# A hybrid mLSTM and stick-breaking attention layer: an earlier weight split, an accumulation inside SBUF, and eight low parts by DMA

## The chip, the cores and the metric

The kernel runs on one core of one Trainium2 chip. The metric is the device time of one execution in microseconds, lower is better. TensorE (PE) multiplies matrices, VectorE (DVE) does arithmetic between tensors, ScalarE (ACT) copies and activations, GpSimd (POOL) smaller work, and SyncE (SP) issues most DMAs. POOL can issue DMAs too, among them accumulating ones, which add what they read to what stands at their destination. Each engine works through its own instructions in the order in which the program was written; semaphores between them make one wait for another.

## What is computed

One layer for 512 tokens of width 1024: an RMS norm, one projection into the columns of two mixers and of two gates, an mLSTM, a stick-breaking attention, two projections, a gated merge, an output projection and the residual. Cut to what matters here:

```python
h = rmsnorm(x, norm_w)
proj = jnp.einsum('bsd,de->bse', h, w_in) + b_in
(mq, mk, mv, mi, mf, mo, mz, sq, sk, sv, sz, gates) = jnp.split(proj, split_at, axis=-1)
...
hm = mlstm_chunkwise(to_heads(mq_c, M_HEADS), to_heads(mk_c, M_HEADS),
                     to_heads(mv, M_HEADS), log_i, log_f)
...
qs = rmsnorm(to_heads(sq, SB_HEADS), sb_q_norm_w)
ks_ = rmsnorm(to_heads(sk, SB_HEADS), sb_k_norm_w)
os_ = stick_breaking_attention(qs, ks_, to_heads(sv, SB_HEADS))
...
merged = (g_m * jnp.einsum('bse,ed->bsd', y_m, w_proj_m)
          + g_s * jnp.einsum('bse,ed->bsd', y_s, w_proj_s))
x = x + jnp.einsum('bsd,de->bse', merged, w_out)
```

## The kernel before

**Split numbers.** A float32 product is made of three matmuls (`mm3`): both factors are split into a high part, rounded to the type that PE reads fast, and a low part, the rest. The names end in h or l: hh and hl of the normed input, wh and wl of a weight. For weights ACT writes the high part by a copy, and DVE the low part by subtracting the high part from the raw weight (`split`, L98 to L100). There is a second way: ACT writes the high part as before (L126) and minus the raw weight, rounded in the same way, into wl (L127), and POOL issues a DMA that adds the raw weight to it in SBUF (L128). A unit takes it if `by_dma` is set, which the last eight units of w_proj_m do.

**Units.** Weights pass in units of 512 KB. The main loop goes over them by number c. At c the two units behind it have been split (`AHEAD`) and the four behind it have been loaded (`LOADS`). Raw units lie in `stg`, a tile of three buffers, so that unit n+3 can be loaded only when unit n's raw weight is no longer read. All of these loads are on SP's queue, in order, and beside them other DMAs, among them the `az<-ay` pieces of an attention head (L542): sixteen small transfers between two tiles, in two groups of eight. A callback with a due number (`later`, `at_unit`, `Pair.at`) is run at the start of its c, ahead of the splits for that c. Engines hold their instructions in the order in which this loop comes to them.

**Which units.** Units 0 to 3 are the first q group. Units 4 to 17 are the first `Pair`, 18 to 31 the second; 32 to 35 a z group, 36 to 39 q and 40 to 43 k of the second set of attention heads, 44 onward the next groups. In the code E is 32.

**Pairs.** A pair makes two 512-column blocks of the projection in seven products instead of eight (Strassen and Winograd), order p = 1, 2, 6, 5, 7, 3, 4, each in two `Half` units g. It holds raw quarters of the weight: X (B11), Z (B21), Y (B12), V (B22). Sums are made in place: `t3` adds B22 to Y by an accumulating DMA out of DRAM (L999), `t2` adds Y to X on DVE (L1004), `t4` adds X to Z (L1008), `t1` subtracts V from X (L1012). X and Y lie in buffers of tag A, four of them, which the attention heads later use for `ay` and `ty`. `Half.split` (L930) splits its quarter, and for p = 1 of the first pair, units 4 and 5, it takes the way by DMA (L936 to L938). Results leave PSUM through ACT (`u`, L1024), DVE (`dst`, L1033) and an accumulating DMA on POOL's queue (`dst<-u`, L1036).

**At the start** ACT also makes copies h of the transposed normed input (L337), sixteen of 128 by 128 for token blocks 2 and 3, from which the forms of the pair are made (L905). Later, in a set of heads, `qraw` and `kraw` are evicted from PSUM by DVE (L387), squared by ACT (`sqj`, L404), and transposed by DVE into `ty` (L431), which takes a buffer of tag A.

Of the kernel before, what the change touches and what calls it, by code (L numbers as in the profile page):

```python
# [12 lines left out]
OP = mybir.AluOpType  # L13
# [14 lines left out]
E = 4 + 14 * PAIRS  # L28
# [9 lines left out]
def tile_hybrid_layer(  # L38
# [16 lines left out]
    nc = tc.nc  # L55
# [21 lines left out]
    def blk(tag, dt=F32, shape=(512,), name=None, p=128):  # L77

        where = mp if tag in MISC else sp
        return where.tile([p] + list(shape), dt, name=name or tag, tag=tag, bufs=BUFS[tag])  # L80
# [17 lines left out]
    def split(src, hi, lo):  # L98
        nc.scalar.activation(hi, src, AF.Copy)  # L99
        nc.vector.tensor_tensor(lo, src, hi.bitcast(F32), op=OP.subtract)  # L100


    class Unit:


        def __init__(self, src, c0, rows=None):
            if rows is None:
                self.ap = src[:, c0:c0 + 128].rearrange("(k p) c -> p k c", p=128)
                self.shape = [KT, 128]
            else:  # L110
                self.ap = src[rows:rows + 256, c0:c0 + 512].rearrange("(k p) c -> p k c", p=128)
                self.shape = [2, 512]
            self.slow = None
            self.heavy = False
            self.by_dma = False
# [5 lines left out]
        def split(self):  # L121
            self.wh = blk("wh", FR, self.shape)
            self.wl = blk("wl", FR, self.shape)
            if self.by_dma:

                nc.scalar.activation(self.wh, self.st, AF.Copy)  # L126
                nc.scalar.activation(self.wl, self.st, AF.Copy, scale=-1.0)  # L127
                nc.gpsimd.dma_start(out=self.wl, in_=self.st, accum_op=OP.add)  # L128
            else:
                split(self.st, self.wh, self.wl)  # L130

    units = []
# [225 lines left out]
    class SbSet:  # L358
# [105 lines left out]
        def head(self, h):  # L464
            hs = slice(h * 128, (h + 1) * 128)
            tr = []
            for name in ("q", "k"):
                th, tl = own = two("qk", FR, name=name + "tt")
                if (name, self.s, h // 2) in TURNED:
                    tp = self.tz[name, h // 2][:, h % 2].rearrange("p a (i j) -> p i a j", j=32)  # L470
                    th, tl = [x.rearrange("p (i a j) -> p i a j", a=4, j=32) for x in own]
                else:
                    tp = att_ps()
                    for tb in range(TB):
                        nc.tensor.transpose(tp[:, tb * 128:(tb + 1) * 128], self.raw[name][tb][:, hs], ident)
                if name == "q" and not (name, self.s, h // 2) in TURNED:
                    nc.scalar.activation(th, tp, AF.Copy, scale=qkw)
                    nc.vector.scalar_tensor_tensor(tl, tp, qkw, th.bitcast(F32), op0=OP.mult, op1=OP.subtract)
                else:
                    split(tp, th, tl)  # L480
                tr.append(own)
# [69 lines left out]
            def turn(js):  # L551
                n0, n1 = slot[js[0], js[0]], slot[TB - 1, js[-1]] + 1
                at = (n1 - n0) * 128
                ah, al = blk("y", FR, name="ath"), blk("y", FR, name="atl")
                split(az[:, :, n0:n1, :].rearrange("p b i j -> p i b j"),
                      *[x[:, 0:at].rearrange("p (i b j) -> p i b j", b=4, j=32) for x in (ah, al)])
                for j in js:
                    o, n = (slot[j, j] - n0) * 128, T - j * 128
                    a_parts[j] = ah[:, o:o + n], al[:, o:o + n]
# [348 lines left out]
    def h_form(row, col):  # L908
        def sta(k, tb):
            c = slice(256 * row + 128 * tb, 256 * row + 128 * tb + 128)  # L910
            return hh[:, 4 * col + k, c], hl[:, 4 * col + k, c]
        return sta

    def s_form(f):
        def sta(k, tb):
            c = slice(128 * tb, 128 * tb + 128)
            return form[f][0][k // 2][:, k % 2, c], form[f][1][k // 2][:, k % 2, c]
        return sta

    class Half:  # L920
# [7 lines left out]
            pass  # L928

        def split(self):  # L930
            self.wh = blk("wh", FR, (2, 512))
            self.wl = blk("wl", FR, (2, 512))
            name = {1: "X", 2: "Z", 6: "X", 5: "X", 7: "Y", 3: "V", 4: "Z"}[self.p]
            x = self.pair.raw[name, self.g]
            if self.pair.base == 4 and self.p == 1:
                nc.scalar.activation(self.wh, x, AF.Copy)  # L936
                nc.scalar.activation(self.wl, x, AF.Copy, scale=-1.0)
                nc.gpsimd.dma_start(out=self.wl, in_=x, accum_op=OP.add)  # L938
            else:
                split(x, self.wh, self.wl)  # L940
# [19 lines left out]
    class Pair:  # L960

        def __init__(self, c1, c2, got1, got2):
            self.c = {1: c1, 2: c2}
            self.got = {1: got1, 2: got2}
            self.raw, self.bank, self.dst = {}, {}, {}
            self.sta = {1: h_form(0, 0), 2: h_form(0, 1), 6: s_form(6), 5: s_form(5),
                        7: s_form(7), 3: s_form(3), 4: h_form(1, 1)}
            b = self.base = len(units)
            for p in (1, 2, 6, 5, 7, 3, 4):
                for g in range(2):  # L970
                    units.append(Half(self, p, g))
            first = b == 4
            for g in range(2):
                if first:
                    plan = {"X": g, "Z": g, "V": 2 + g, "Y": 1}
                else:
                    plan = {"X": b - 8 + g, "Z": b - 8 + 6 * g, "V": b - 4 + g, "Y": b - 6 + g}
                for name, c in plan.items():
                    self.at(c, self.load, name, g)
                self.at(b + g - 1 if first else b + g - 3, self.t3, g)  # L980
                self.at(b + 1 + g, self.t2, g)
                self.at(b + 3 + g, self.t4, g)
                self.at(b + 4 + g, self.t1, g)
            self.at(b + 1, self.rows)
# [10 lines left out]
            nc.sync.dma_start(t, w_in[r:r + 256, c:c + 512].rearrange("(k p) c -> p k c", p=128))  # L995

        def t3(self, g):
            r, c = 512 + 256 * g, self.c[2]
            nc.gpsimd.dma_start(out=self.raw["Y", g], accum_op=OP.add,  # L999
                                in_=w_in[r:r + 256, c:c + 512].rearrange("(k p) c -> p k c", p=128))  # L1000

        def t2(self, g):
            x, y = self.raw["X", g], self.raw["Y", g]
# [60 lines left out]
    def at_unit(c, fn, *a):  # L1064
        later.setdefault(c, []).append(lambda: fn(*a))

    for f in (5, 7, 6):
        for i in range(2):
            at_unit(2, form_sum, f, i)
# [124 lines left out]

    chan_group(w_proj_m, 0, D, lambda k: ymp[k], pm_evac)
    n_proj = len(units)
    for un in units[n_proj - 8:]:
        un.by_dma = True


# [170 lines left out]
    for g in range(2):  # L1371
        at(-15 + 2 * g, w_load, "B22", g, "P5")
        at(-14 + 2 * g, w_load, "B12", g, "A")
        at(-11 + 2 * g, w_load, "B11", g, "A")
        at(-11 + 2 * g, t3, g)
        at(-7 + 2 * g, t2, g)
        at(-6 + 2 * g, t1, g)
        at(1 + g, t4, g)
# [115 lines left out]
    for c in range(N):  # L1494
# [34 lines left out]
        for e in list(pend):  # L1529
            if c >= e[0] and e[2]():  # L1530
                pend.remove(e)
                g = e[3]()
# [36 lines left out]
```

## Time and profile before

| | |
|---|---|
| median of 3 runs | 705.02 us (703.99 to 705.18) |
| the profiled execution | 705.31 us, its span 703.6 us |
| mean granted clock of PE | 0.988 of full speed |
| HBM read, written | 71.46 MB, 5.30 MB |
| 76 low parts on DVE (wl<-stg) | 93.0 us busy, 1224 ns each |
| 8 low parts by DMA (wl<-stg) | 5.9 us from issue to landing, median |

In a list of waits a row has the engine, what waited and its line, an arrow to what ended the wait, and then the total in us, how often, and the longest. In a timeline a row begins with the start and the length in us, and a bracket at its end says how long the engine had been idle and what ended that. A window has the busy time of PE, the granted clock (PEclk), the DMA share, and GB/s; the share is packet time over the time of sixteen engines, and goes past 1 where packets overlap.

### The profile page before, as it was taken

Reading aid. Unit: us, or ns where it says so; the run is one execution under the profiler, and the core shown is the slowest. Engines: PE = TensorE matmul, PEld = TensorE weight load, DVE = VectorE, ACT = ScalarE, POOL = GpSimd, SP = SyncE. Lnnn points to the kernel's source line nnn. Section 1 sums busy time; section 2 is a strip of 40 time slices with the busy share of each in tenths; the row PEclk is TensorE's granted clock in tenths of the full one; section 3 lists DMA queues with packets and bytes.
Section 4 is the critical chain, followed back from the end, with each engine's and each line's share of the span. In section 5 each row is a group of like instructions: output and inputs, shape, how many; then the busy total and the mean of one; then the engine's idle time right before and its main releaser. Section 6 shows DMA issues by size and latency. Waiting matters only on the chain.

```text
span 703.6 us, 9522 instructions
## 1 busy us (share of the span) xinstructions
PE 681.4 (97%) x3114; PEld 563.8 (80%) x3114; DVE 499.0 (71%) x857; ACT 367.7 (52%) x697; POOL 147.5 (21%) x308
## 2 busy tenths in 40 slices
PE   8988989999979999999999999999999999999997
PEld 5866867888768888888887888888888888888876
DVE  6858678787686876698998446599734365545896
ACT  7656436654736554564445664444647452444461
POOL 4023416542545421130001031100001200111020
PEclk9989999999998999999999999999999999999999
DMA  6775965735343456525455424334432335989433
GB/s 245 262 143 152 247 169 116 186 87 173 81 125 97 115 177 178 155 61 150 92 101 143 134 61 120 82 101 133 109 101 69 92 118 148 301 182 220 129 79 102
DMA packets 127666, 97.33 MB, mean 138 GB/s; under 512 B 19658, under 2 KB 105060, under 8 KB 127616
## 3 DMA queue, kind: packets, MB, share of 16 engines
q1 hardware_dynamic: 121104, 83.48, 41.7%
q0 software_dynamic: 6368, 13.11, 10.0%
q8 instruction: 24, 0.39, 0.2%
q14 instruction: 26, 0.21, 0.1%
q10 hardware_dynamic: 144, 0.13, 0.1%
HBM read 71.46 MB, written 5.30 MB: 109 GB/s over the span
## 4 chain that ended last, share of the span: by engine, by line
PE 64%; DVE 9%; issue 5%; DMA 4%; ACT 3%; SPq 2%; POOL 1%; DVEq 0%; POOLq 0%; ACTq 0%
PE dps L94 17%; PE dps L96 17%; PE dps L95 17%; PE aps L95 2%; PE aps L96 2%; PE aps L94 2%; DVE acc L724 2%; SPq L542 2%; DMA Y<-in_w_in_dram 2%; PE dps L953 2%; DVE wl L100 1%; DMA stg<-in_w_in_dram 1%; PE aps L953 1%; ACT sqj L404 1%; DVE tmp L730 1%
## 5 line engine op out<-in xcount | busy, mean ns | idle before, releaser
L94 PE MATMUL dps<-hh,wh 128*128 128x512 f32 x448 | 176.6, 394 | 5.1 <-DVE kraw L387 4.5
L96 PE MATMUL dps<-hh,wl 128*128 128x512 f32 x448 | 175.5, 392 | 0.6 <-DVE wl L100 0.6
L95 PE MATMUL dps<-hl,wh 128*128 128x512 f32 x448 | 175.3, 391 | 0.0
L100 DVE TENSOR_TENSOR wl<-stg,wh 128x1024 fp32r<-128x1024 f32 x76 | 93.0, 1224 | 65.3 <-ACT wh L99 64.8
L94 PEld LDWEIGHTS dps<-hh,wh 128*128 128x128 f32 x448 | 84.7, 189 | 22.4 <-issue 4.9
L96 PEld LDWEIGHTS dps<-hh,wl 128*128 128x128 f32 x448 | 84.6, 189 | 19.4 <-DVE wl L100 1.4
L99 ACT ACTIVATE wh<-stg 128x1024 fp32r<-128x1024 f32 x76 | 80.0, 1052 | 37.9 <-PE dps L95 11.2
L95 PEld LDWEIGHTS dps<-hl,wh 128*128 128x128 f32 x448 | 84.8, 189 | 16.8
L94 PE MATMUL dps<-wh,hh 128*128 128x512 f32 x96 | 37.6, 392 | 1.3 <-DVE qraw L387 1.3
L727 ACT ACTIVATE tmp<-acc 128x512 f32<-128x512 f32 x16 | 10.1, 633 | 52.3 <-DVE acc L724 52.3
L96 PE MATMUL dps<-wh,hl 128*128 128x512 f32 x96 | 37.4, 390 | 0.0
L95 PE MATMUL dps<-wl,hh 128*128 128x512 f32 x96 | 37.4, 390 | 0.0
L724 DVE SCALAR_TENSOR_TENSOR acc<-tmp,vec,acc 128x511 f32<-128x511 f32 (+2 forms) x48 | 36.0, 750 | 1.7
L500 POOL TENSOR_SCALAR_AFFINE_SELECT om<-om 128x128 f32<-128x128 f32 x32 | 14.1, 439 | 83.6 <-ACT om L498 83.6
L786 POOL TENSOR_SCALAR_AFFINE_SELECT w_all<-om 128x128 f32<-128x128 f32 x16 | 7.4, 492 | 109.2 <-DMA om<-rb_d 109.1
L506 DVE TENSOR_TENSOR_SCAN om<-om 128x512 f32<-128x512 f32 (+3 forms) x32 | 26.6, 831 | 4.4 <-POOL om L500 4.4
L441 POOL DMA_DIRECT2D tz<-ty x48 | 25.9, 549 | 9.2 <-PE aps L953 5.0
L96 PE MATMUL dps<-yh,wl 128*128 128x512 f32 x64 | 25.0, 390 | 0.0
L95 PE MATMUL dps<-yl,wh 128*128 128x512 f32 x64 | 24.9, 389 | 0.0
L94 PE MATMUL dps<-yh,wh 128*128 128x512 f32 x64 | 24.9, 389 | 0.0
L498 ACT ACTIVATE om<-aps,rq 128x512 f32<-128x512 f32 (+3 forms) x32 | 16.9, 527 | 13.3 <-PE aps L96 12.2
L843 ACT ACTIVATE hns<-aps,hst 128x256 f32<-128x256 f32 x16 | 7.6, 475 | 29.8 <-DVE hst L842 22.6
(303 smaller groups left out, 1553.1 us busy)
## 6 DMA issues: line engine op xcount, KB each, us to landing
stg<-in_w_in_dram SPq DMA_DIRECT2D x71, 512.0 KB
az<-ay SPq DMA_DIRECT2D x128, 40.0 KB
stg<-in_w_proj_s_dram SPq DMA_DIRECT2D x8, 512.0 KB
B<-in_w_out_dram SPq DMA_DIRECT2D x8, 512.0 KB
stg<-in_w_proj_m_dram SPq DMA_DIRECT2D x8, 512.0 KB
wl<-stg POOLq DMA_DIRECT2D x8, 512.0 KB, 5.9
dst<-u POOLq DMA_DIRECT2D x12, 256.0 KB, 5.7
X<-in_w_in_dram SPq DMA_DIRECT2D x4, 512.0 KB
```

The costliest lines, as they stand in the source:

```text
L94: nc.tensor.matmul(ps, ah, bh, start=first, stop=False)
L95: nc.tensor.matmul(ps, ah, bl, start=False, stop=False)
L96: nc.tensor.matmul(ps, al, bh, start=False, stop=last)
L99: nc.scalar.activation(hi, src, AF.Copy)
L100: nc.vector.tensor_tensor(lo, src, hi.bitcast(F32), op=OP.subtract)
L441: q.dma_start(tz[32 * b:32 * b + 32, :, a, :], src[32 * a:32 * a + 32, b])
L498: nc.scalar.activation(om[:, 0:n], zp, AF.Sigmoid, scale=rn[:, h:h + 1])
L500: nc.gpsimd.affine_select(out=om[:, ts], in_=om[:, ts], compare_op=OP.is_gt, fill=1.0, base=0, channel_multiplier=1, pattern=[[-1, 128]])
L506: nc.vector.tensor_tensor_scan(back, back, back, 1.0, op0=OP.mult, op1=OP.bypass)
L542: nc.sync.dma_start(az[32 * a:32 * a + 32, b, :, :], ay[32 * b:32 * b + 32, a, :, :])
L724: nc.vector.scalar_tensor_tensor(acc[:, j:], t[:, 0:T - j], cw(3 - j, ch), acc[:, j:], op0=OP.mult, op1=OP.add)
L953: nc.tensor.matmul(pr.bank[key, tb], a, w[:, i, :], start=begin and n == 0, stop=end and n == 2, skip_group_check=again)
```

## The change

It has three parts.

1. `Half.split` does nothing if it has been done. The splits of units 4 and 5 are asked for by callbacks at c = 1 and c = 2.
2. `t3` adds V to Y inside SBUF in place of B22 out of DRAM. For this the first pair loads V at c = g, with X and Z, and not at c = 2 + g; and `t3` is due at b + g - 2 in both pairs: units 2 and 3 in the first (before 3 and 4), units 16 and 17 in the second (before 15 and 16).
3. Units E+4 to E+11, that is 36 to 43, take the way by DMA for their low parts.

```diff
         def split(self):
+            if hasattr(self, "wh"):
+                return
             self.wh = blk("wh", FR, (2, 512))
...
-                    plan = {"X": g, "Z": g, "V": 2 + g, "Y": 1}
+                    plan = {"X": g, "Z": g, "V": g, "Y": 1}
...
-                self.at(b + g - 1 if first else b + g - 3, self.t3, g)
+                self.at(b + g - 2, self.t3, g)
...
         def t3(self, g):
-            r, c = 512 + 256 * g, self.c[2]
-            nc.gpsimd.dma_start(out=self.raw["Y", g], accum_op=OP.add,
-                                in_=w_in[r:r + 256, c:c + 512].rearrange("(k p) c -> p k c", p=128))
+            nc.gpsimd.dma_start(out=self.raw["Y", g], in_=self.raw["V", g], accum_op=OP.add)
...
+    for g in range(2):
+        at_unit(1 + g, units[4 + g].split)
...
-    for un in units[n_proj - 8:]:
+    for un in units[n_proj - 8:] + units[E + 4:E + 12]:
         un.by_dma = True
```

Where it moves instructions is seen in the engines' own order. First ACT near the start, before the change; L337 are the h copies (the last eight rows of two are those of token blocks 2 and 3), L936 and L937 the split of a unit of the first pair:

```order
L337 ACTIVATE h_356<-aps,nw_t 128x128 x2
L337 ACTIVATE h_359<-aps,nw_t 128x128 x2
L936 ACTIVATE wh<-X 128x1024
L937 ACTIVATE wl<-X 128x1024
L936 ACTIVATE wh<-X 128x1024
L937 ACTIVATE wl<-X 128x1024
```

and ACT in the same place of the changed kernel, where these lines are L938 and L939:

```order
L337 ACTIVATE h_286<-aps,nw_t 128x128 x2
L337 ACTIVATE h_289<-aps,nw_t 128x128 x2
L938 ACTIVATE wh<-X 128x1024
L939 ACTIVATE wl<-X 128x1024
L337 ACTIVATE h_349<-aps,nw_t 128x128 x2
L337 ACTIVATE h_352<-aps,nw_t 128x128 x2
...
L337 ACTIVATE h_365<-aps,nw_t 128x128 x2
L337 ACTIVATE h_368<-aps,nw_t 128x128 x2
L938 ACTIVATE wh<-X 128x1024
L939 ACTIVATE wl<-X 128x1024
```

Unit 4's two copies now stand ahead of the sixteen h copies of token blocks 2 and 3; unit 5's stand behind them, where unit 4's stood.

POOL from the first pair to the second, as a difference (rows of the norms between them left out); `wl<-X` are the low parts of units 4 and 5, `Y<-` the accumulations of `t3`, `dst<-u` those of the pairs' results:

```order
-L938 DMA wl<-X 128x1024 x2
-L999 DMA Y<-in_w_in_dram 128x2x512 x2
...
-L1036 DMA dst<-u 128x512 x2
-L999 DMA Y<-in_w_in_dram 128x2x512
-L1036 DMA dst<-u 128x512 x2
-L999 DMA Y<-in_w_in_dram 128x2x512
...
+L940 DMA wl<-X 128x1024
+L1000 DMA Y<-V 128x1024
+L940 DMA wl<-X 128x1024
+L1000 DMA Y<-V 128x1024
...
+L1036 DMA dst<-u 128x512 x4
+L1000 DMA Y<-V 128x1024 x2
```

In the first pair one `Y<-V` now stands ahead of unit 5's low part; in the second pair both stand behind four `dst<-u`, where each stood behind two.

The third place is DVE at units 42 and 43 (k of the second set), before the change; `wl` is a unit's low part, `ay`, `om` and `a_all` belong to an attention head:

```order
L387 TENSOR_TENSOR qraw<-dps,brow 128x512 x4
L100 TENSOR_TENSOR wl<-stg,wh 128x1024
L100 TENSOR_TENSOR qtt<-tz,qtt 128x512
L100 TENSOR_TENSOR ktt<-tz,ktt 128x512
L100 TENSOR_TENSOR wl<-stg,wh 128x1024
L524 STREAM_TRANSPOSE ay<-a_all 128x4x32 x5
```

and POOL at the same place of the changed kernel, where the two low parts are now issued; L282 to L411 are the norms of q:

```order
L411 TENSOR_SCALAR rq<-rq 128x4
L128 DMA wl<-stg 128x1024
L282 TENSOR_SCALAR rq<-ssq 128x4
L283 TENSOR_TENSOR rq<-rq,mhalf 128x4
L411 TENSOR_SCALAR rq<-rq 128x4
...
L128 DMA wl<-stg 128x1024
L499 MEMSET om 128x1
```

Both `wl` rows are gone from DVE. SP's order around units 42 and 43 is the same before and after: a load, eight `az<-ay`, a bias row, a load, eight `az<-ay`; what frees the `stg` buffer of each load is now the end of a low part's DMA instead of a DVE instruction.

## The prediction

> **What bounds the kernel now.** I read the page's head first, then the list of what TensorE (PE) waited for, then the timelines of the engines around each wait.
>
> ```profile
> span 703.6 us, 9522 instructions
> PE 681.4 (97%) x3114; PEld 563.8 (80%) x3114; DVE 499.0 (71%) x857; ACT 367.7 (52%) x697; POOL 147.5 (21%) x308
> PE dps L94 <- DVE kraw L387: 4.5, 1, 4.5
> PE aps L953 <- DVE wl L100: 3.7, 3, 2.4
> PE dps L953 <- DMA wl<-X: 2.9, 1, 2.9
> PE dps L953 <- DVE wl L100: 1.0, 2, 0.8
> ```
>
> PE is busy for 97% of the span, and the change takes no matmul away. So the time can move only at PE's few holes: what each lasts, and what it does to the clock afterwards. The rows (total, times, longest) say what ended the largest: one wait of 4.5 us for VectorE (DVE) evicting kraw, three of 3.7 us together for low parts made on DVE, one of 2.9 us for a low part made by DMA, and two of 1.0 us together for DVE again. I call the places gap 1 (the DMA, at 36 us), gap 2 (58 us, DVE low parts), gap 3 (97 to 108 us, several short ones, second pair) and gap 4 (kraw, 206 us). All sums are against the profiled execution, 705.31 us (span 703.6 and 1.7 around it); it lies 0.3 above the median of 705.02. 0.2% of it, 1.4 us, is about what a measurement of this kernel can tell from no change.
>
> **Gap 1: unit 4's low part (edit 1).** Rows of ACT, of POOL, of PE, and PE's windows (busy, granted clock, DMA share, GB/s):
>
> ```profile
> 24.51 1.14 ACT L337 ACTIVATE h<-aps,nw_t 128x128 f32<-128x128 f32 x4 [3.60 <-DVE hl L325]
> 29.79 1.15 ACT L337 ACTIVATE h<-aps,nw_t 128x128 f32<-128x128 f32 x4 [0.61 <-DVE hl L325]
> 30.80 1.08 ACT L936 ACTIVATE wh<-X 128x1024 fp32r<-128x1024 f32 x1
> 31.75 1.07 ACT L937 ACTIVATE wl<-X 128x1024 fp32r<-128x1024 f32 x1
> 33.15 1.04 POOL L938 DMA_DIRECT2D wl<-X  x1 [16.18 <-ACT wl L937]
> 35.23 0.39 PE L1448 MATMUL dps<-fl,hh 128*128 128x512 f32 x1
> 35.46 0.39 PE L953 MATMUL dps<-wh,hh 128*128 128x512 f32 x1
> 38.77 0.80 PE L953 MATMUL dps<-wl,hh 128*128 128x512 f32 x1 [2.93 <-DMA wl<-X]
> 37.00:38.00 1.00, 0.00 (x0) 0.96 0.93 172
> 38.00:39.00 1.00, 0.23 (x1) 0.50 1.10 197
> 44.00:45.00 1.00, 1.00 (x4) 0.63 1.05 236
> ```
>
> Unit 4's split (L936, L937) stands behind sixteen h copies, so its DMA leaves at 33.15 and lands at about 38.7. Matmuls follow each other by 0.23 us: PE could have gone on at 35.46 + 0.23 = 35.69 and went on at 38.77, 3.1 us later. The clock fell just before 38.0 and was still 0.63 on average in the last window shown: full speed from 44.74. The 6.0 us from 38.77 to 44.74 ran at half speed, another 3.0 lost. **Gap 1 costs about 6.0 us.**
>
> The move puts unit 4's two copies into ACT's idle 3.60 us before 24.51. X of half 0 must be in by then:
>
> ```profile
> DMA packets 1521, 2.94 MB, mean 294 GB/s; under 512 B 98, under 2 KB 98, under 8 KB 1519
> GB/s 410 467 410 377 369 385 385 385 410 410 401 418 426 401 385 393 393 385 410 401 434 418 393 393 418 401 393 254 197 172 98 49 25 33 25 16 0 0 0 0
> ```
>
> This is 24 to 34 us in forty slices: the pair's eight loads of 0.52 MB run at about 400 GB/s, 1.3 us each, until 31. Of their 4.2 MB some 1.3 had moved before 24, so X0, first in the queue, is there by about 24. The copies then end by 26, and the h copies, which before waited 0.6 us between groups for DVE, absorb the rest. The DMA leaves at about 26 and takes, amid loads, 5.6 us as before or somewhat more: 32 to 34.5, ahead of 35.69. That hole closes.
>
> What is late next is unit 5. Its split now stands directly behind the h copies, where unit 4's stood: copies 30.8 to 32.8, DMA at 33.15. Unit 5 starts on PE at 35.46 + 12 x 0.227 = 38.2 and needs its low part one matmul later, at 38.4. With the 5.6 us of gap 1's DMA it lands at 38.75; it now has Y<-V of half 0 ahead of it on POOL's queue, and the second one behind it, so I let it land between 38.7 and 40.2, and take a wait of 1.0. No hole of PE of 1.5 us or less in this trace is followed by half clock. **Gain 5.0 us**, between 3.5 (wait of 2.5, clock still full) and 6.0 (no wait).
>
> The Trainium skill, "TensorE: Matmul & The Clock Gate", section "What's actually happening", has the clock fall after at least one idle window, about 3.4 us. By that rule gap 1, idle for 2.9, would never have lost its clock, would cost 3.1 alone, and the sum below would come out 2.9 us higher. The trace disagrees: 0.50 stands in the window from 38.00 after 2.3 us of idleness, so I go by the rows.
>
> **Gap 2 (nothing).** This chain is DVE's own:
>
> ```profile
> 50.82 1.23 DVE L100 TENSOR_TENSOR wl<-X,wh 128x1024 fp32r<-128x1024 f32 x1 [0.26 <-ACT wh L99]
> 60.11 1.22 DVE L100 TENSOR_TENSOR wl<-X,wh 128x1024 fp32r<-128x1024 f32 x1
> ```
>
> Between the two DVE has no idle time; the work is timed by unit 6's start, not by Y's arrival. It moves as a block with PE: 0, apart from 1.5 either way for where half clock falls. V0 and V1 loaded earlier delay X1 by one load, 1.3 us, to about 29, still ahead of its split at 30.8. The removed DRAM read of Y's addend is 2 MB less traffic over both pairs and no time by itself.
>
> **Gap 3 (edit 2 in the second pair).** The chain of waits and the rows around it:
>
> ```profile
> 81.59 13.13 DMA Y<-in_w_in_dram
> 94.82 1.23 DVE L1004 TENSOR_TENSOR X<-X,Y 128x1024 f32<-128x1024 f32 x1 [4.38 <-DMA Y<-in_w_in_dram]
> 76.57 1.89 POOL L999 DMA_DIRECT2D Y<-in_w_in_dram  x1
> 80.45 1.78 POOL L1036 DMA_DIRECT2D dst<-u  x2 [2.00 <-DVE dst L1033]
> 89.00:91.00 2.00, 2.00 (x10) 1.00 1.15 220
> ```
>
> The second accumulation takes 13.1 us and holds DVE for 4.4, which costs PE at least 2.3 us in short holes (the 3.7 of the list without gap 2's 2.4, and the 1.0). Reading from SBUF spares the DRAM side, and the packets are larger. But both accumulations now stand behind all four dst<-u, so the first leaves at about 81.6, not 76.57, and both then share a DMA system that is full (share 1.15). The second lands between 92.8 and 96 against 94.73. I take 0.3 gained; bounds: 2.3 gained (all that PE pays for), 1 lost (landing at 96).
>
> **Gap 4: eight low parts by DMA (edit 3).** Rows of DVE, SP, PE and ACT, then how the late stage, which already does this, fares:
>
> ```profile
> 186.02 1.22 DVE L100 TENSOR_TENSOR wl<-stg,wh 128x1024 fp32r<-128x1024 f32 x1 [2.59 <-ACT wh L99]
> 187.27 0.37 SPq L119 DMA_DIRECT2D stg<-in_w_in_dram  x1
> 187.75 4.97 SPq L542 DMA_DIRECT2D az<-ay  x8
> 193.44 0.39 SPq L119 DMA_DIRECT2D stg<-in_w_in_dram  x1
> 193.88 5.28 SPq L542 DMA_DIRECT2D az<-ay  x8
> 200.55 1.42 DVE L431 STREAM_TRANSPOSE ty<-qraw 128x256 f32<-128x256 f32 x4 [1.48 <-DMA az<-ay]
> 209.95 2.48 DVE L387 TENSOR_TENSOR kraw<-dps,brow 128x512 f32<-128x512 f32 x4
> 210.78 0.76 PE L94 MATMUL dps<-hh,wh 128*128 128x512 f32 x1 [4.50 <-DVE kraw L387]
> 184.94 1.04 ACT L99 ACTIVATE wh<-stg 128x1024 fp32r<-128x1024 f32 x1
> L127 ACT ACTIVATE wl<-stg x8: 1041/1041/1047, 607.6 to 645.7; 128x1024 fp32r<-128x1024 f32 x8
> DMA to landing us min/median/max: 4.8/5.9/8.9
> SPq L119 <- DMA wl<-stg: 29.2, 5, 6.9
> ```
>
> Eight DVE subtractions of 1.22 go, 9.8 us, but PE waits for none of them; eight ACT copies of 1.04 and eight DMAs come. What matters is the stg slot: the load three units on takes it when the low part is done, now when the DMA **lands**. On SP's queue that load stands ahead of the az pieces, and DVE's ty reuses the buffer that those pieces read; DVE waited 1.48 us for them and then ran without a break to kraw, for which PE waited 4.5. The chain SP, az, ty, kraw, PE has no slack left.
>
> Step by step: unit 42's high part ends at 185.98, its negative copy about 1.0 later, its DMA leaves at 187.35 and lands 4.8 to 5.9 later, at 192.1 to 193.2. The load that stood at 187.27 slips by 4.9 to 5.9. The eight az issues follow (5.0), brow (0.6), and the second load, which then finds unit 43's DMA (copies end at 193.1, landing at 198.3 to 199.4) just done. The whole row slips by 5 to 6 us, ty with it, and PE restarts at about 216.4 instead of 210.78: **5.6 lost**, bounds 5.0 and 6.5. The eight DMAs themselves come in time: unit 42 is needed at 194.1, unit 43 at 200. In the late stage SP lost 29.2 us in five such waits, up to 6.9 each, so the wait is real. The longer hole also leaves the clock down: on average 0.2 more.
>
> ACT takes the eight copies between 150 and 193, where it is idle for whole waits; were that cover gone, unit 42's DMA would leave a copy, 1 us, later, and the slip would be 6.6.
>
> **Sum:** 705.3 - 5.0 (gap 1) + 0 (gap 2) - 0.3 (gap 3) + 5.6 + 0.2 (gap 4) = 705.8 in a profiled execution, 705.5 beside the median.
>
> **The rivals.**
> - *Forecast, 0.45:* gap 1's gain is eaten by gap 4. Its own range is 703.0 to 708.5: faster 0.07, same 0.22, slower 0.16.
> - *Early and light transfers win, 0.27:* unit 5's DMA, at the shortest landing, misses nothing (6.0 gained instead of 5.0), and SBUF accumulation empties the queue, so gap 3 goes too (2.3 instead of 0.3). 705.5 - 1.0 - 2.0 = 702.5, down to 701 if the az pieces slip only by 4. For it: a 512 KB low part took 4.8 us where traffic was light. Against it: DMA share above 1 where both sit. All faster.
> - *Unit 5 breaks the clock again, 0.20:* its DMA shares POOL's queue with Y<-V and the remaining loads. If it lands later than about 40.5, PE idles for over 2 us as before and half clock follows; gap 1 returns 1 to 2 us in place of 5.0, and the time is 709 to 710. For it: Y<-in took 9.6 to 13.1 us in that queue. All slower. The Trainium skill, "DMA: Bandwidth & Descriptors", section "Queues, rings and completion order", says that an engine takes turns between queue rows by packet, so the loads would not merely go first; no row here shows the turns.
> - *Edit 2 doesn't do what it says, 0.08:* the second accumulation lands after 96, since it now shares the queue with the first from its start; gap 3 grows by 1 to 2, 707 to 708. Slower 0.06, same 0.02.
>
> For that 13.1 and the 9.6:
>
> ```profile
> DMA to landing us min/median/max: 9.6/11.3/13.1
> ```
>
> Chances: faster 0.07 + 0.27 = 0.34, same 0.22 + 0.02 = 0.24, slower 0.16 + 0.20 + 0.06 = 0.42. The range runs from 700.0 to 710.5: it leaves out the corners, unit 42 at the 8.9 us landing (PE itself would wait and the row slip by 9) and at the lower end it goes a little past the faster rival's 701.
>
> **What would show it.** Right: no half clock between 38 and 45 us, and a wait of about 1 us or less at unit 5's first low matmul; DVE's first X<-X,Y of the second pair later than 87.6 relative to unit 18; SP waiting at L119 for a wl<-stg landing near 188 (all 5 us earlier by the clock), az and ty 5 to 6 us later against PE's unit 42, and a kraw wait near 10 us. Wrong: PE's kraw wait stays near 4.5, or the clock falls in the first pair, or gap 3's holes are gone.

## The result and the profile after

| | before | after |
|---|---|---|
| median, runs on the same chips | 704.50 us (703.75 to 705.38, n = 6) | 708.33 us (707.26 to 709.90, n = 6) |
| profiled execution, its span | 705.31 us, 703.6 us | 707.75 us, 706.0 us |
| ratio after / before | | 1.0056 (95%: 1.004 to 1.0072) |

The change makes the kernel slower by 0.56%, 0.40 to 0.72%; the forecast was 705.5 us with a range of 700.0 to 710.5. Ratios here are estimated from all timed executions and can differ a little from the quotient of the medians; one execution of e4 below, at 1130.1 us, is left out of its ratio. The list of PE's waits in the changed kernel (total, times, longest), to be held against the one of before:

```profile
PE dps L94 <- DVE kraw L387: 10.4, 1, 10.4
PE aps L955 <- DVE wl L100: 3.8, 3, 2.4
PE dps L955 <- DMA wl<-X: 2.2, 1, 2.2
```

Gap 4 grew from 4.5 to 10.4 us. The wait for a low part by DMA in the first pair is still there, 2.2 instead of 2.9 us, but it is now unit 5's. The two waits of 1.0 us on L953's DVE low parts are gone from the list, and gap 2's row is nearly as it was (before 3.7 us in three waits, now 3.8).

Gap 1 in the changed kernel, POOL's and PE's timelines and one of PE's windows (busy, granted clock, DMA share, GB/s):

```profile
25.45 1.06 POOL L940 DMA_DIRECT2D wl<-X  x1 [8.84 <-ACT wl L939]
28.27 0.87 POOL L1000 DMA_DIRECT2D Y<-V  x1 [1.75 <-DMA Y<-in_w_in_dram]
33.07 0.85 POOL L940 DMA_DIRECT2D wl<-X  x1 [3.93 <-ACT wl L939]
35.45 0.39 PE L955 MATMUL dps<-wl,hh 128*128 128x512 f32 x1
40.53 0.50 PE L955 MATMUL dps<-wl,hh 128*128 128x512 f32 x1 [2.20 <-DMA wl<-X]
41.00:42.00 1.00, 1.00 (x6) 1.00 0.93 190
```

Unit 4's low part is in time: its first low matmul runs at 35.45 without a wait. Unit 5's DMA leaves at 33.07 as forecast, but is in only at about 40.5, 7.4 us later. The clock stays at 1.00 behind that wait in this execution.

Gap 4, SP's, DVE's and PE's timelines and SP's list of waits:

```profile
188.76 5.91 SPq L542 DMA_DIRECT2D az<-ay  x8
195.40 0.37 SPq L119 DMA_DIRECT2D stg<-in_w_in_dram  x1
195.82 5.40 SPq L542 DMA_DIRECT2D az<-ay  x8
202.62 1.42 DVE L431 STREAM_TRANSPOSE ty<-qraw 128x256 f32<-128x256 f32 x4 [5.59 <-DMA az<-ay]
212.84 0.76 PE L94 MATMUL dps<-hh,wh 128*128 128x512 f32 x1 [10.37 <-DVE kraw L387]
SPq L119 <- DMA wl<-stg: 51.9, 10, 9.2
```

PE runs 3.8 us earlier than before when it reaches this stage, and yet the first az group leaves 1.0 us later (188.76 against 187.75) and the second 1.9 later. DVE's ty waits 5.59 us for them, before 1.48. SP's waits for a low part's landing have grown from 5 to 10 and from 29.2 to 51.9 us.

Gap 3, DVE's timeline:

```profile
87.40 1.23 DVE L1004 TENSOR_TENSOR X<-X,Y 128x1024 f32<-128x1024 f32 x1 [2.86 <-DMA Y<-V]
91.00 1.23 DVE L1004 TENSOR_TENSOR X<-X,Y 128x1024 f32<-128x1024 f32 x1 [1.24 <-DMA Y<-V]
```

The first X<-X,Y now waits as well (2.86 us), the second less (1.24, before 4.38). PE's lead over the kernel of before grows from 3.0 to 3.8 us over gap 3.

Matmul by matmul the starts in the two profiled executions differ by: -5.7 us after gap 1's place, -3.5 after unit 5's wait, -3.0 after gap 2, -3.8 after gap 3, +2.1 after gap 4, and +2.4 at the last one.

### The profile page after: what moved, and what is told of

Read it like the earlier page. It is cut to its first block, busy times and chain, and to the rows that moved or that the text cites. A ratio compares the mean times of both kernels' runs of the same rounds, so it can differ in the third digit from the quotient of the medians.

```text
span 706.0 us, 9541 instructions
## 1 busy us (share of the span) xinstructions
PE 678.5 (96%) x3114; PEld 562.3 (80%) x3114; DVE 490.1 (69%) x849; ACT 375.6 (53%) x705; POOL 151.8 (21%) x316
## 3 DMA queue, kind: packets, MB, share of 16 engines
q1 hardware_dynamic: 121104, 83.48, 40.5%
## 4 chain that ended last, share of the span: by engine, by line
PE 62%; DVE 9%; DMA 7%; issue 5%; ACT 4%; SPq 2%; POOL 0%; DVEq 0%; ACTq 0%; POOLq 0%
PE dps L96 17%; PE dps L94 17%; PE dps L95 17%; PE aps L95 2%; PE aps L96 2%; PE aps L94 2%; DMA wl<-stg 2%; DVE acc L724 2%; DMA stg<-in_w_in_dram 2%; DMA Y<-V 2%; SPq L542 2%; PE dps L955 2%; DVE wl L100 1%; PE aps L955 1%; DMA az<-ay 1%
## 5 line engine op out<-in xcount | busy, mean ns | idle before, releaser
L94 PE MATMUL dps<-hh,wh 128*128 128x512 f32 x448 | 176.5, 394 | 10.9 <-DVE kraw L387 10.4
L100 DVE TENSOR_TENSOR wl<-stg,wh 128x1024 fp32r<-128x1024 f32 x68 | 83.4, 1226 | 56.1 <-ACT wh L99 55.7
L99 ACT ACTIVATE wh<-stg 128x1024 fp32r<-128x1024 f32 x68 | 71.6, 1052 | 29.4 <-PE dps L95 10.9
L94 PE MATMUL dps<-wh,hh 128*128 128x512 f32 x96 | 37.6, 392 | 1.3 <-DVE qraw L387 1.3
L128 POOL DMA_DIRECT2D wl<-stg x16 | 14.3, 892 | 94.5 <-DVE yml L100 40.0
L126 ACT ACTIVATE wh<-stg 128x1024 fp32r<-128x1024 f32 x16 | 16.9, 1058 | 28.4 <-PE dps L95 16.9
L500 POOL TENSOR_SCALAR_AFFINE_SELECT om<-om 128x128 f32<-128x128 f32 x32 | 16.0, 506 | 58.3 <-ACT om L498 58.1
```

Of the source, the lines that this page charges most:

```text
L94: nc.tensor.matmul(ps, ah, bh, start=first, stop=False)
L500: nc.gpsimd.affine_select(out=om[:, ts], in_=om[:, ts], compare_op=OP.is_gt, fill=1.0, base=0, channel_multiplier=1, pattern=[[-1, 128]])
```

## The experiments

Nine kernels, each against the kernel of before on the same chip. The medians of before beside them were 703.2 to 703.9 us, so ratios are compared, not microseconds from one comparison to another. Column "unit 5" is PE's wait for unit 5's low part (in the kernels without edit 1, unit 4's), "kraw" the wait at gap 4, both in the profiled execution.

| kernel | ratio to before (95%) | unit 5 | kraw |
|---|---|---|---|
| changed kernel | 1.0056 (1.004 to 1.0072) | 2.2 | 10.4 |
| e1: edits 1 and 2 | 0.9974 (0.9959 to 0.9989) | 2.3 | 4.8 |
| e2: edit 3 alone | 1.0099 (1.008 to 1.0117) | 2.1 | 10.4 |
| e3: edit 1 alone | 0.9959 (0.9945 to 0.9973) | none | 4.4 |
| e4: all, six units by DMA | 0.9979 (0.9966 to 0.9991) | 2.0 | 5.0 |
| e5: e1, Y<-V behind both low parts | 0.9948 (0.9935 to 0.9960) | none | 4.6 |
| e6: all, unit 42 only | one execution, 707.29 us | 2.2 | 9.7 |
| e7: all, unit 43 only | one execution, 709.10 us | 1.8 | 9.9 |
| e8: all, az pieces first | 0.9998 (0.9984 to 1.0012) | 2.2 | 5.7 |
| e9: e5, az pieces first | 0.9915 (0.9899 to 0.9932) | none | 3.1 |

**e1, the first two edits.** Against the changed kernel:

```diff
-    for un in units[n_proj - 8:] + units[E + 4:E + 12]:
+    for un in units[n_proj - 8:]:
```

> Edits 1 and 2 without edit 3 (units 36 to 43 keep their low parts on DVE). Theory S (edit 3 costs through SP's queue: the load three units on waits for the landing, the az pieces stand behind it): the kraw wait returns from 10.4 to about 4.5 us and the time is 3.5 to 4.5 us under before, 0.994 to 0.995. Rival D (the lengthened kraw wait comes from the earlier edits, since everything ahead of it runs 3.8 us earlier and DVE or the transfers do not follow): the kraw wait stays at 8 us or more and the time is within 0.2% of before.

The kraw wait is 4.8 us, so its growth comes from edit 3 and not from what runs ahead of it; D falls. The profiled span is 700.4, 3.2 under the profiled one of before, but by the ratio the gain is only 0.26%, 1.8 us, about half of what was expected. Its twelve executions spread from 699.3 to 704.3; e4 and e5 below bear on that.

**e2, edit 3 alone** (the same line the other way, on the kernel of before).

> Edit 3 alone on the kernel of before. Theory S: the kraw wait is 10 to 10.5 us, the gaps of the pairs are as before, and the time is 5.5 to 6.5 us over before, 1.008 to 1.009. Rival D: the kraw wait is below 6 us and the time within 0.3% of before.

10.4 us and 1.0099: S, by the ratio a little above the 1.009 that it expected, by the medians (6.05 us over before) inside. Edit 3 alone loses more than the whole change does. This run also shows how much gap 1 varies: its first pair is that of the kernel of before, and yet PE waited 2.08 us there and not 2.93, and half clock lasted 3.4 us and not 6.8 (37.6 to 41.0, against 37.9 to 44.7). Reckoned as in the prediction, gap 1 cost some 4 us in this execution and not 6.0.

**e3, edit 1 alone.** The guard in `Half.split` and the two `at_unit` calls on the kernel of before, with both accumulations behind both low parts on POOL's queue.

> Edit 1 alone: the early split of unit 4, the accumulations still out of DRAM and, on POOL's queue, behind both low parts. Theory Q (unit 5's 2.2 us wait in the changed kernel comes from the Y<-V that shares the queue ahead of its low part): unit 5's low part lands at 38.7 to 39.5, PE waits 0.3 to 1.0 us there, and the time is 5 to 6 us under before, 0.992 to 0.993. Rival L (the loads still in flight delay it): the wait stays near 2 us and the time is about 3.5 us under before, 0.995.

Unit 5's wait is gone: the low part was issued at 32.79 and landed 5.7 us later (the shortest in the view of tile X), in time. So the wait follows Q. The gain is 0.41%, less than the 0.7 to 0.8% expected, and the traces show two things that took from it. A hole opens 10 us on: unit 8's low part on DVE comes 1.02 us late, behind an X<-X,Y before which DVE had stood idle (the profile names no releaser there; its Y, summed out of DRAM, is the likely one):

```profile
48.49 0.50 PE L955 MATMUL dps<-wl,form 128*128 128x512 f32 x1 [1.02 <-DVE wl L100]
```

And the 5 to 6 us were taken from one profiled execution of before, of 705.3 us, in which gap 1 cost 6.0; the median of before beside e3 is 703.2, and e2's execution shows gap 1 at some 4. e3's five times, 699.4 to 700.5, lie close together.

**e4, six units by DMA.** Against the changed kernel:

```diff
-    for un in units[n_proj - 8:] + units[E + 4:E + 12]:
+    for un in units[n_proj - 8:] + units[E + 4:E + 10]:
```

> The changed kernel with six units by DMA, 36 to 41, and units 42 and 43 on DVE again. Theory S (only the two loads that stand ahead of the az pieces matter, those that wait for units 42 and 43): the kraw wait is 4 to 5 us, and the time is that of edits 1 and 2 alone within 0.2%. Rival G (each of the eight DMAs costs its share, by ACT's copies or by the DMA engines): three quarters of the loss stays, some 4 us over edits 1 and 2 alone.

The kraw wait is 5.0, the ratio that of e1 within 0.05%. Units 36 to 41 by DMA cost nothing and bring nothing that these runs can tell; G falls as a share of each unit. This kernel's profiled execution also shows what the 2 us hole at unit 5 can do. PE's timeline, and PE's windows:

```profile
40.32 0.50 PE L955 MATMUL dps<-wl,hh 128*128 128x512 f32 x1 [1.98 <-DMA wl<-X]
41.00:42.00 1.00, 1.00 (x4) 0.50 1.11 223
```

Here 1.98 us of idleness was followed by half clock, in the changed kernel 2.20 us was not. The kernels with this hole spread (e1 5.0 us over twelve executions, e8 4.3 over twelve), those without it less (e3 1.1 over five, e5 1.7 over six, e9 2.3 over five). Fewer executions spread less in any case, so this is a hint and no proof.

**e5, the order on POOL.** Against e1:

```diff
-                self.at(b + g - 2, self.t3, g)
+                self.at(b + g - 1 if first else b + g - 2, self.t3, g)
```

> Edits 1 and 2 without edit 3, the first pair's Y<-V put behind both low parts on POOL's queue (due one unit later). Theory Q (the Y<-V ahead of it delays unit 5's low part): the 2 us wait at unit 5 is gone, the low part lands within 6.5 us of its issue, and the time is that of edit 1 alone or up to 1.5 us under it (699 to 700.5; its later hole near 48 us closes where Y<-V lands earlier than the DRAM form). Rival L (loads still in flight): the wait stays 1.5 us or more and the time is that of edits 1 and 2.

POOL's timeline (the low part of unit 5, then the first Y<-V) and PE's next wait:

```profile
33.09 0.85 POOL L940 DMA_DIRECT2D wl<-X  x1 [6.26 <-ACT wl L939]
33.64 1.18 POOL L1000 DMA_DIRECT2D Y<-V  x1
47.76 0.50 PE L955 MATMUL dps<-wl,form 128*128 128x512 f32 x1 [0.62 <-DVE wl L100]
```

The low part left at 33.09, as in the changed kernel (33.07), and was in after 5.3 us instead of 7.4. The loads were still in flight here too: their queue moved 0.46 MB from 32 to 36 us, in the changed kernel 0.26. So the Y<-V issued at 28.27 ahead of it, not the loads, made it late in the changed kernel. The median, 699.46, is 0.5% under before, in the band that Q named; the later hole shrank from 1.02 to 0.62 us.

**e6 and e7, one unit by DMA.** `units[E + 10:E + 11]` and `units[E + 11:E + 12]` in the changed kernel's line.

> The changed kernel with the DMA way for unit 42 alone of the eight. Theory S: the load that waits for unit 42 slips about 5 us and everything behind it on SP with it, so the kraw wait is 9 to 10.5 us, nearly all of the loss from one unit. Rival H (the two waits add up, each half): 7 to 8 us. Rival G (ACT's copies): below 5.5.

> The changed kernel with the DMA way for unit 43 alone of the eight. Theory S: the second load, between the two groups of az pieces, waits for unit 43's landing, 4.5 to 5 us after the time at which it stood, and the second group with it: kraw wait 8.5 to 10 us, by itself nearly the whole loss again. Rival H: 7 to 8 us. Rival G: below 5.5.

Rows of the lists of PE's waits, e6 and then e7:

```profile
PE dps L94 <- DVE kraw L387: 9.7, 1, 9.7
PE dps L94 <- DVE kraw L387: 9.9, 1, 9.9
```

Either unit alone makes nearly all of the loss, and both together hardly more: the costs are not a sum. (That is read from the waits; each kernel has one timed execution.) SP's timeline of e7 shows how:

```profile
190.79 0.58 SPq L350 DMA_DIRECT2D brow<-in_b_in_dram  x1
197.02 0.37 SPq L119 DMA_DIRECT2D stg<-in_w_in_dram  x1
197.44 5.02 SPq L542 DMA_DIRECT2D az<-ay  x8
```

With unit 42 on DVE the first group leaves early, SP is through at 191.4, and then stands until 197.0 for unit 43's landing. With unit 42 by DMA it is the first load that stands, and when SP comes to the second, unit 43 is nearly done.

**e8, the az pieces first.** The two loads that wait for units 42 and 43 are issued after the head's generators of their c. Against the changed kernel:

```diff
-        fetch(c + LOADS + 1)
+        if c not in LATE:
+            fetch(c + LOADS + 1)
+
+    LATE = (E + 9, E + 10)
...
+        if c in LATE:
+            fetch(c + LOADS + 1)
         units[c].mm(1)
```

> The changed kernel, all eight by DMA, with the two loads that wait for units 42 and 43 issued behind the az pieces that stood behind them. Theory S: ty no longer waits for az, the kraw wait falls from 10.4 to 3 to 4 us, below the 4.5 of before, and the time is 6 to 8 us under the changed kernel, 700.5 to 702.5. Rival G (the DMAs' traffic or ACT's copies make the loss): the kraw wait stays at 9 us or more and the time with it. What could spoil it: the later loads miss units 45 and 46, which would show as new PE waits on wl L100 or L99 near 215 us.

SP's, DVE's and PE's timelines:

```profile
179.79 4.96 SPq L542 DMA_DIRECT2D az<-ay  x8
189.62 6.84 SPq L542 DMA_DIRECT2D az<-ay  x8
197.95 1.43 DVE L431 STREAM_TRANSPOSE ty<-qraw 128x256 f32<-128x256 f32 x4 [0.87 <-DMA az<-ay]
208.18 0.77 PE L94 MATMUL dps<-hh,wh 128*128 128x512 f32 x1 [5.67 <-DVE kraw L387]
```

The kraw wait falls from 10.4 to 5.7 with all eight DMAs in place, and the time by 0.6% against the changed kernel (0.9998 over 1.0056); no new wait shows near 215 us. So the order on SP is the main mechanism. But 3 to 4 us were expected, and ty waits 0.87 only. Most of what is left is not az: the last a_all on DVE, after which ty can run, ends 5.4 us before PE runs dry (197.1 and 202.5), in the kernel of before 7.2 (199.1 and 206.3). In the changed kernel too it is 5.4.

**e9, without edit 3.** e5 with the loads of e8.

> Edits 1 and 2 with the Y<-V behind both low parts, no edit 3, and the loads that wait for units 42 and 43 behind the az pieces. Theory S with ACT's share: with az in time and no second ACT copy ahead of the attention scores, ty runs as soon as DVE reaches it and the kraw wait is about 3.0 us (4.5 less the 1.5 that ty waited for az before), where the same order with all eight by DMA had 5.7; the time is 697.5 to 698.5 us, 0.992 to 0.994, under all others. Rival: the wait at 5.7 us came from the order of loads itself, and stays at 5 us or more here, with 700 us or more.

DVE's and PE's timelines:

```profile
193.03 1.42 DVE L431 STREAM_TRANSPOSE ty<-qraw 128x256 f32<-128x256 f32 x4
203.26 0.47 PE L94 MATMUL dps<-hh,wh 128*128 128x512 f32 x1 [3.15 <-DVE kraw L387]
```

ty waits for nothing, the kraw wait is 3.1, and a_all again ends 7.2 us before PE runs dry (192.9 and 200.1). So some 1.8 us of e8's wait came from elsewhere than az. Two things stand ahead of that head's scores under edit 3: on ACT the second copies of units 42 and 43, after each of which the next instruction starts 0.95 us later, and on POOL the issue of their DMAs, ahead of its masks, which are slower there as well (last section). ACT's timeline of e8 at unit 43, and DVE's and PE's of e6, where unit 42 alone goes by DMA:

```profile
188.32 1.04 ACT L127 ACTIVATE wl<-stg 128x1024 fp32r<-128x1024 f32 x1
189.27 0.45 ACT L498 ACTIVATE om<-aps,rq 128x256 f32<-128x256 f32 x1
195.80 0.29 DVE L507 TENSOR_TENSOR a_all<-a_all,om 128x128 f32<-128x128 f32 x1
212.05 0.77 PE L94 MATMUL dps<-hh,wh 128*128 128x512 f32 x1 [9.71 <-DVE kraw L387]
```

In e6 the masks are as fast as without any of the eight (0.29 us), and still a_all ends 6.2 us before PE runs dry (196.1 and 202.3), 1.0 less than without edit 3: one copy. In e7 it is 6.2 as well, with slow masks. Two copies, 1.9 us, cover the whole 1.8, so ACT's copies are the cause and the masks add nothing that shows. At 0.9915 e9 is the fastest of all, 0.7 to 1.0% under before.

## Why the prediction came out as it did

The time lay inside the range, and the main account held: a gain in the first pair, more than eaten by SP's hold-up at units 42 and 43. That the range held it says little: it was 10.5 us wide, and the times of seven of the nine experiments lie in it too. Of the signs that the prediction named, those for gaps 3 and 4 came; a wait of 1 us or less at unit 5 did not (2.2), and half clock in the first pair, a sign of being wrong, is absent from the changed kernel's profile but stands in those of four of the five experiments with the same first pair and that hole (e4, e6, e7, e8, not e1). So the outcome lies between the forecast and its rival "unit 5 breaks the clock again". The likeliest case was too optimistic by 3.3 us on the forecast's difference of +0.5 to before (measured +3.8 between medians), and same or faster had together a larger chance than slower.

- **Gap 1, unit 4 (right).** The copies went to 23.1 to 25.1 us, the DMA left at 25.45, and the low part was not late.
- **Gap 1, unit 5 (the term that was mis-sized).** "I let it land between 38.7 and 40.2, and take a wait of 1.0" measured 7.4 us from issue, landing at 40.5, a wait of 2.2; the gain was 3.5 in the profiled execution, not 5.0. The duration was taken from gap 1's own DMA, 5.6 us, which had no accumulation ahead of it. e5 shows that the Y<-V ahead is what was missing: 5.3 us without it. The rival had put the point of decision at 40.5, where it landed: the clock fell in some executions (e4's profile) and not in others (the changed kernel's), and that it held in the profiled one was luck.
- **"Gap 1 costs about 6.0 us" (true of one execution).** It is the sum over the profile of before. With the same instructions e2's profile shows some 4, half clock for 3.4 us instead of 6.8; e3, which closes the hole, gained 0.41%, 2.9 us.
- **"No hole of PE of 1.5 us or less is followed by half clock" (right, and of no help).** The hole that came was longer. The 2.3 us after which the clock of before had fallen is no threshold either: it fell after 1.84 us in e7 and held after 2.33 in e1.
- **Gap 2 (right).** Its wait is 2.4 before and after. The lead shrinks there by 0.5, with half clock after it for 6.8 us instead of 3.4, within the 1.5 that the prediction left for this.
- **Gap 3 (right, 0.8 instead of 0.3, inside the bounds).** The first accumulation was late and made DVE wait, as forecast; only it was put further back on POOL's queue, as the second stood behind all four dst<-u before too. The second landed at 90.9, 12.0 after its issue; with PE's lead of 3.0 added that is 93.9, inside the bounds of 92.8 and 96 and 0.8 ahead of before. Of the 2.3 us that the prediction puts down to the second accumulation only 0.8 were its: the two waits of together 1.3 us on aps in the second pair are as long in the changed kernel, and 0.2 stood at 66 us, in the first pair.
- **Gap 4 (right).** 5.6 forecast with bounds of 5.0 and 6.5; 5.9 measured. The steps held too: both loads stood for landings, az, ty, kraw and PE followed one for one. One part was counted as hidden and is not quite: the copies of units 42 and 43 delay that head's scores, as e8 and e9 bring to light. Behind az it was not visible.
- **The clock after gap 4 (sign wrong, small).** Forecast 0.2 lost. The longer hole did leave the clock down for longer, 10.2 us instead of 6.8, but most of that fell into the hole itself: after PE's restart half clock lasted 4.2 us (212.8 to 217.0) instead of 4.6 (210.8 to 215.4), 0.2 less lost.
- **The profiled execution as the base of the sum.** The difference of the two profiled executions is +2.4 us. The medians' +3.8 adds 1.4, in keeping with half clock at unit 5 in some executions (3.4 us of it, 1.7 lost, in e4's profile), which the profiled one did not pay. No profile of a slower execution of the changed kernel shows it.

## What to carry to other kernels

Moving an instruction's work to a DMA frees an engine but lengthens the life of what the DMA reads: look first for who waits for that buffer, and for what stands behind that waiter on its queue. Here two of eight DMAs made the loss, and either alone made nearly all of it. In a queue that one engine works through in order, put what the bottleneck waits for ahead of what has time: two loads put later on SP and one accumulation on POOL took e1 to e9, 0.9974 to 0.9915, as much as all three edits together had lost.

## What the runs showed of the hardware

An accumulating DMA inside SBUF slows the ordinary loads beside it. The changed kernel's DMA queues from 32 to 36 us, where q0 carries Y<-V and unit 5's low part, and q1 the rest of the pair's loads (packets, MB, share of 16 engines' time):

```profile
q0 software_dynamic: 194, 0.70, 87.5%
q1 hardware_dynamic: 140, 0.26, 19.8%
```

Per packet that is 289 ns on q0 (0.875 of 16 engines in 4 us, over 194) against 91 ns on q1. Loads that in the kernel of before, without such DMAs beside them, were through by 33 us took much longer. The second Y<-V waits for the last of them, and in e1, which has the same first pair, it could be issued only at 41.1:

```profile
41.09 0.85 POOL L1000 DMA_DIRECT2D Y<-V  x1 [8.09 <-DMA Y<-in_w_in_dram]
```

In e4 it was 38.97, with the same releaser, and in the changed kernel 39.84, where the row names a DVE instruction. In e5, where the first Y<-V comes later, the second left at 36.52. The Trainium skill, "DMA: Bandwidth & Descriptors", section "Queues, rings and completion order", has an engine take turns between queue rows by packet. 194 against 140 packets is not far from turns, and by turns the queue with the longer packets takes the larger part of the time; no run here sets this apart from another rule.

POOL's own work is slower right behind a DMA that it issues. POOL's timeline of the changed kernel, right after unit 43's DMA, and of e5, where that low part is on DVE:

```profile
190.80 0.94 POOL L500 TENSOR_SCALAR_AFFINE_SELECT om<-om 128x128 f32<-128x128 f32 x1
```

```profile
187.71 0.29 POOL L500 TENSOR_SCALAR_AFFINE_SELECT om<-om 128x128 f32<-128x128 f32 x1
```

The same instruction takes 0.94 and 0.29 us. It takes 0.94 in e2 and e8 and 0.63 in e7, which issue unit 43's DMA there too, and 0.29 in e6, where only unit 42's was issued, six us earlier. Spans on POOL are rough, and what slows it stays open.

How long PE is idle does not decide alone whether the clock falls. The hole at the low part by DMA in the first pair, and the half clock that followed it in each profile:

| | idle, us | half clock, us |
|---|---|---|
| before, e2 (unit 4) | 2.93, 2.08 | 6.8, 3.4 |
| changed kernel, e1 (unit 5) | 2.20, 2.33 | none, none |
| e4, e6, e7, e8 (unit 5) | 1.98, 2.22, 1.84, 2.22 | 3.4 each |

Gap 2's hole, 2.4 us in every profile, was followed by 3.4 us of half clock in the kernel of before, by 6.8 in the changed kernel and by none in e1. All these lengths are multiples of 3.4 us. The Trainium skill, "TensorE: Matmul & The Clock Gate", section "What's actually happening", gives a window that runs freely, which agrees with a fall that depends on where the hole lies, and at least one idle window of about 3.4 us before it, with which the 1.84 to 2.22 us do not agree.
